# A two-layer encoder trunk: reads for a half's second part queued behind the weights, activations rounded behind their weight tile, one activation table loaded later

## The chip, the cores and the metric

One core of one Trainium2 chip. The metric is the device time of one execution in microseconds (us). The program is built by a tile framework whose scheduler decides, from a timeline of its own, in which order each engine's instructions stand; `issue_after(x)` in the source adds the condition that what follows stands behind `x` in time. What the scheduler made of the source is shown below where it matters.

## The reference

`x` is 512 tokens of 1024 floats. Layer 0 mixes by a convolution and a gated linear attention, layer 1 by softmax attention with forget gates; each layer ends with a PEER expert block, which is where most of the work is:

```python
def peer_ffn(h, wq, keys, u, v):              # h: 512 x 1024, u and v: 16384 x 1024
    q = h @ wq                                # 8 heads, two halves of 128
    s1, s2 = q[..., 0, :] @ keys[:, 0], q[..., 1, :] @ keys[:, 1]
    v1, i1 = top_k(s1, 16); v2, i2 = top_k(s2, 16)
    sc, j = top_k(v1[:, None] + v2[None, :], 16)          # 16 experts a head, 128 a token
    experts, gates = i1[j // 16] * 128 + i2[j % 16], softmax(sc)
    act = gelu(u[experts] . h)
    return sum(gates * act * v[experts])
```

`x = x + mix(rms_norm(x))` and `x = x + peer_ffn(rms_norm(x))` in each of the two layers.

## The kernel before, in words

The program runs `mix_even`, `peer(0)`, `mix_odd` and `peer(1)` one after the other. Each `peer` treats 128 tokens (block 0) by gathering the rows of `u` and `v` that its tokens chose, and the other 384 tokens densely: for all 16384 experts, in 128 tiles of 128.

The dense part has two halves. The **u half** (`u_step`, L842) loads a weight tile of 128x1024 floats, computes 24 matmuls into a PSUM bank `pu`, takes the gelu of it, and keeps the 128x384 activations: the last 24 tiles in SBUF (`act0` to `act23`), the first 104 in DRAM (`aside`). Beside it `gate4` builds the tokens' gates and writes them to DRAM as `G`. The **v half** (`prepare`, L962, and `v_sweep`, L1022) takes each tile's gates (`gc`, read from `G` for 8 tiles at once) and activations (kept, or `at`, read from `aside` for 2 tiles at once), multiplies them on VectorE (L971), and uses the product as the stationary operand of 18 matmuls with the weight tile of `v`.

Every operand in float32 is split into two float32r parts (`split`, L49): ScalarE rounds it (`whi` for a weight, `wh` for the gated activations, both L50), and VectorE (in places GpSimd) takes the rest (`wlo`, `wl`, both L51). Buffers: 4 `raw` weight tiles in flight, 3 each of `whi`, `wlo`, `wh`, `wl`, 2 of `gc`, 3 of `at`. All weight loads (L58), `gc` (L957) and `at` reads (L960) go through one queue, SP's, in one order.

The v half's order of experts is such that the 24 kept tiles come first. When the u half's last gates are done (about 12 tiles before its end), `upool` is closed, the pools of the v half are opened, and `fetch` (L950) is called for the first tiles: that asks for two `gc` and three `at` reads at once. Inside the loop it is called four tiles ahead.

Gathers go on in both halves on GpSimd's queue (L861 and L872); VectorE takes their dot products (L863) and later their weighted sum (L874). When the last dot product is there, `g_w` (L866) takes its gelu on ScalarE.

`mix_odd` begins with a request to load ScalarE's table set that holds both exp and ln (L545), placed behind `last_gelu`, which is `g_w`'s gelu. In the attention, `log_sigmoid` (L206 to L218) uses exp (L211) and ln (L215), `rsqrt` (L223, L224) ln and then exp, and the softmax exp (L645). `sums_in` (L588) transposes the result of `log_sigmoid`, `fz`, on TensorE (L590); `normalise` (L617) ends in `ka` or `qa` (L627), which the logits (L639) need.

Of the kernel before, what the change touches and what calls it, by code (L numbers as in the profile page):

```python
# [39 lines left out]
TAIL = 12  # L40
NEG = -3.0e38
# [3 lines left out]
class Trunk:  # L45
# [8 lines left out]
    def weight(self, src, shape=None, eng=None, after=None):  # L54

        nc = self.nc
        raw = self.ws.tile([P, D], F32, tag="raw", name="raw", bufs=4)
        nc.sync.dma_start(raw, src)  # L58
        hi = self.ws.tile([P, D], F32R, tag="whi", name="whi", bufs=3)
        lo = self.ws.tile([P, D], F32R, tag="wlo", name="wlo", bufs=3)  # L60
        if after:
            with self.tc.issue_after(after.ins):
                self.split(raw, hi, lo, eng)
        else:
            self.split(raw, hi, lo, eng)
        if shape:
            a, b = shape
            hi = hi.rearrange("p (a b) -> p a b", a=a)
            lo = lo.rearrange("p (a b) -> p a b", a=a)
        return hi, lo  # L70
# [471 lines left out]
    def mix_odd(self):  # L542
        nc, tc, A = self.nc, self.tc, self.A
        with tc.issue_after(self.last_gelu.ins):
            nc.scalar.preload_act_table_set("natural_log_exp_and_others")  # L545
        hT = self.new_hT()
        with tc.tile_pool(name="m1c", bufs=1) as sc:
            start, rest = self.nat_parts(A["w_v1"][0], self.rows(hT), 2, eng=nc.gpsimd)
            self.rms_h(2, hT, after=start)
            self.mix_odd_body(hT, sc, rest)  # L550
# [263 lines left out]
    def peer_body(self, L, hT, h0, sp, sb):  # L814
# [27 lines left out]
        def u_step(e, eng=None):  # L842
# [10 lines left out]
            self.last_gelu = nc.scalar.activation(a, p, AF.Gelu)  # L853
# [96 lines left out]
        def fetch(n):  # L950
# [3 lines left out]
            if m % EC == 0 and m < NE1:  # L954
                e = order[m]
                gcs[m] = vb.tile([P, NTG, EC * TG], F32, name="gc")
                nc.sync.dma_start(gcs[m], G[:, :, e * TG:(e + EC) * TG].rearrange("g p n -> p g n"))  # L957
            if 0 <= n < NE1 and (e := order[n]) < NE1 - KEEP and n % 2 == 0:
                ats[n] = vb.tile([P, 2, TD], F32, name="at", bufs=3)
                nc.sync.dma_start(ats[n], aside[e:e + 2].rearrange("e p t -> p e t"))  # L960

        def prepare(n):  # L962
# [5 lines left out]
            lo = self.last_lo  # L968
# [5 lines left out]
            self.split(w, *[t.rearrange("p (g t) -> p g t", t=TG) for t in (wh, wl)])  # L974
# [13 lines left out]
        while nu < NE1:  # L988
# [15 lines left out]
            if not (gates or products or vb):  # L1004
                upool.__exit__(None, None, None)
                vb = vpool.__enter__()
                for n in range(-AHEAD, AHEAD):
# [52 lines left out]
    def build(self, stop=4, first=0):  # L1060
        nc, tc, A = self.nc, self.tc, self.A
        with tc.tile_pool(name="const", bufs=1) as cp, tc.tile_pool(name="ws", bufs=1) as self.ws, \
# [13 lines left out]
            self.last_gelu = nc.vector.memset(sc[:, 0:1], -0.5)  # L1076
# [97 lines left out]
```

## Time and profile before

| | us |
|---|---|
| median of 3 runs | 3146.25 (3145.14 to 3149.17) |
| the profiled execution | 3148.14 |
| its span, from the first instruction to the last | 3146.3 |
| TensorE busy in the span | 3080.9 |
| VectorE, ScalarE, GpSimd busy | 2406.8, 1437.2, 1155.1 |
| moved by DMA | 787.16 MB, 250 GB/s on average |

All times in rows are from the start of the span. Layer 0's u half ends at about 1012 us, its v half at 1540, the attention at 1868; layer 1's u half ends at 2609, its v half at 3138. PE is TensorE, DVE VectorE, ACT ScalarE, POOL GpSimd, SPq the queue of DMA issues on SyncE. A row of idle time names what the engine's next instruction waited for last.

### The profile page before, as it was taken

What the parts mean: (1) busy time and instruction counts of PE and PEld (TensorE: products, weight loads), DVE (VectorE), ACT (ScalarE), POOL (GpSimd) and SP (SyncE); (2) the same over time, 40 slices, a digit from 0 to 9 for tenths busy, and PEclk for the clock granted to TensorE, in tenths of its full rate; (3) what the DMA queues carried; (4) which work ended last, traced back from release to release, by engine and by line L of the source; (5) the groups of instructions that cost most, each with busy time, mean ns of one, the idle gap of its engine ahead of it and who ended that gap; (6) DMA issues with size and microseconds to landing.
All of it is one profiled execution on the core that took longest, in us unless ns stands there. A gap on an engine that the chain in (4) does not pass through costs nothing.

```text
span 3146.3 us, 45733 instructions
## 1 busy us (share of the span) xinstructions
PE 3080.9 (98%) x15932; PEld 2696.8 (86%) x15932; DVE 2406.8 (76%) x4936; ACT 1437.2 (46%) x2258; POOL 1155.1 (37%) x800
## 2 busy tenths in 40 slices
PE   8999999999999999999999999999999999999999
PEld 6668999999999888877766679999999998888787
DVE  6765998888885888888535548998888867888786
ACT  4343334666664333333356633336666643333332
POOL 1220122996773332332100000227976752233330
PEclk9999999999999999999999999999999999999999
DMA  4113445999998999999421124448999997999996
GB/s 155 54 34 125 137 140 168 358 351 347 339 323 292 310 350 372 352 350 356 148 81 41 41 77 132 137 144 313 375 340 339 339 322 260 354 367 346 355 349 233
DMA packets 334202, 787.16 MB, mean 250 GB/s; under 512 B 26745, under 2 KB 181770, under 8 KB 327826
## 3 DMA queue, kind: packets, MB, share of 16 engines
q1 hardware_dynamic: 260242, 515.76, 47.0%
q0 software_dynamic: 73728, 268.47, 24.1%
q8 instruction: 125, 2.05, 0.3%
q14 instruction: 107, 0.88, 0.1%
HBM read 687.59 MB, written 96.47 MB: 249 GB/s over the span
## 4 chain that ended last, share of the span: by engine, by line
PE 90%; DVE 3%; DMA 2%; issue 1%; ACT 1%; SPq 1%; POOL 1%; DVEq 0%; ACTq 0%; POOLq 0%
PE acc L1027 33%; PE pu L79 10%; PE pu L78 10%; PE pu L77 10%; PE bank L77 5%; PE bank L79 5%; PE bank L78 5%; PE bank L911 5%; PE po L671 1%; PE pc L284 1%; PE bank L639 1%; PE bank L935 1%; DVE wlo L51 1%; SPq L960 1%; POOL gr L861 1%
## 5 line engine op out<-in xcount | busy, mean ns | idle before, releaser
L50 ACT ACTIVATE whi<-raw 128x1024 fp32r<-128x1024 f32 x604 | 636.9, 1057 | 829.5 <-PE pu L78 471.6
L51 DVE TENSOR_TENSOR wlo<-raw,whi 128x1024 fp32r<-128x1024 f32 x565 | 692.1, 1226 | 183.1 <-ACT whi L50 156.3
L77 PE MATMUL pu<-hhi,whi 128*128 128x384 f32 x2048 | 702.0, 343 | 9.6 <-ACT whi L50 8.7
L79 PE MATMUL pu<-hhi,wlo 128*128 128x384 f32 x2048 | 691.0, 338 | 2.2 <-DVE wlo L51 2.2
L78 PE MATMUL pu<-hlo,whi 128*128 128x384 f32 x2048 | 689.2, 337 | 0.0
L872 POOL DMA_INDIRECT gr<-in_vF_dram,ids x256 | 317.7, 1241 | 717.7 <-DVE x L874 658.7
L1027 PE MATMUL acc<-wlo,wh 128*128 128x512 f32 x1536 | 472.7, 389 | 0.0
L1027 PE MATMUL acc<-whi,wl 128*128 128x512 f32 x1536 | 472.5, 389 | 0.0
L1027 PE MATMUL acc<-whi,wh 128*128 128x512 f32 x1536 | 436.5, 390 | 9.3 <-ACT whi L50 9.3
L861 POOL DMA_INDIRECT gr<-in_uN_dram,ids x256 | 352.5, 1377 | 237.6 <-DVE dots L863 140.7
L50 ACT ACTIVATE wh<-gc 128x384 fp32r<-128x384 f32 x256 | 134.4, 525 | 645.7 <-PE acc L1027 638.0
L77 PEld LDWEIGHTS pu<-hhi,whi 128*128 128x128 f32 x2048 | 388.3, 190 | 12.1 <-ACT whi L50 9.3
L79 PEld LDWEIGHTS pu<-hhi,wlo 128*128 128x128 f32 x2048 | 387.3, 189 | 4.0 <-DVE wlo L51 3.9
L78 PEld LDWEIGHTS pu<-hlo,whi 128*128 128x128 f32 x2048 | 388.1, 190 | 1.9 <-DVE hlo L117 0.6
L1027 PEld LDWEIGHTS acc<-whi,wh 128*128 128x128 f32 x1536 | 287.6, 188 | 72.1 <-ACT whi L50 12.6
L1027 PEld LDWEIGHTS acc<-wlo,wh 128*128 128x128 f32 x1536 | 288.3, 188 | 60.0
L1027 PEld LDWEIGHTS acc<-whi,wl 128*128 128x128 f32 x1536 | 288.3, 188 | 59.8
L901 POOL TENSOR_SCALAR a<-cst,sT 128x128 f32<-128x128 f32 x192 | 330.6, 1722 | 13.2 <-PE bank L911 4.9
L874 DVE SCALAR_TENSOR_TENSOR x<-gr,dots,x 128x1024 f32<-128x1024 f32 x256 | 327.4, 1279 | 0.3
L863 DVE CUSTOM_DVE_ANT_0 gr<-gr,h 128x1024 f32<-128x1024 f32 x256 | 307.9, 1221 | 23.8 <-DMA gr<-in_uN_dram,ids 23.7
L51 DVE TENSOR_TENSOR wl<-gc,wh 128x384 fp32r<-128x384 f32 x256 | 142.7, 558 | 179.4 <-ACT wh L50 170.0
L51 POOL TENSOR_TENSOR wlo<-raw,whi 128x1024 fp32r<-128x1024 f32 x39 | 99.0, 2540 | 398.5 <-ACT whi L50 390.5
(248 smaller groups left out, 4242.3 us busy)
## 6 DMA issues: line engine op xcount, KB each, us to landing
raw<-in_uT_dram SPq DMA_DIRECT2D x256, 512.0 KB
raw<-in_vF_dram SPq DMA_DIRECT2D x256, 512.0 KB
G<-big SPq DMA_DIRECT2D x48, 1024.0 KB
gc<-G SPq DMA_DIRECT2D x32, 1536.0 KB
aside<-xact SPq DMA_DIRECT2D x208, 192.0 KB
at<-aside SPq DMA_DIRECT2D x104, 384.0 KB
raw<-in_w_in_dram SPq DMA_DIRECT2D x32, 512.0 KB
raw<-in_wq_dram SPq DMA_DIRECT2D x32, 512.0 KB
```

The source lines that it names most:

```text
L50: first = self.nc.scalar.activation(hi, raw, AF.Copy)
L51: self.last_lo = (eng or self.nc.vector).tensor_tensor(lo, raw, hi.bitcast(F32), op=ALU.subtract)
L77: mm(out, lh, rh, start=first, stop=False)
L78: mm(out, lh, rl, start=False, stop=False)
L79: return mm(out, ll, rh, start=False, stop=last)
L861: nc.gpsimd.indirect_dma_start(out=r, out_offset=None, in_=uN, in_offset=bass.IndirectOffsetOnAxis(ap=ids[:, s:s + 1], axis=0))
L863: return lambda: nc.vector.tensor_tensor_reduce(r, r, h0, 1.0, 0.0, ALU.mult, ALU.add, accum_out=dots[:, s:s + 1])
L872: nc.gpsimd.indirect_dma_start(out=r, out_offset=None, in_=vF, in_offset=bass.IndirectOffsetOnAxis(ap=ids[:, s:s + 1], axis=0))
L874: return lambda: nc.vector.scalar_tensor_tensor(self.x0, r, dots[:, s:s + 1], self.x0, op0=ALU.mult, op1=ALU.add)
L901: (nc.vector if t else nc.gpsimd).tensor_scalar(a1[:, t], self.iota, e1[:, t:t + 1], gate[:, t:t + 1], op0=ALU.is_equal, op1=ALU.mult)
L911: nc.tensor.matmul(p[:, t], a2[:, t], a1[:, t], start=True, stop=True)
L1027: nc.tensor.matmul(acc[b][c], wt[:, s], vt[:, c], start=(n == 0 and wt is wh and vt is vh), stop=(n == NE1 - 1 and wt is wl))
```

## The change

Three things are done. `fetch` is called seven tiles later than the pools are opened (`SETTLE`), and each `gc` and `at` read is asked to stand behind the last weight load issued by then. The split of the gated activations (`wh`, `wl`) is asked to stand behind the rounding of its own tile's weights. The table set of the attention is asked to be loaded behind the u half's last gelu (`last_act`) as well as behind `g_w`'s.

```diff
+SETTLE = 7
...
         raw = self.ws.tile([P, D], F32, tag="raw", name="raw", bufs=4)
-        nc.sync.dma_start(raw, src)
+        self.last_raw = nc.sync.dma_start(raw, src)
...
         if after:
             with self.tc.issue_after(after.ins):
-                self.split(raw, hi, lo, eng)
+                self.last_hi = self.split(raw, hi, lo, eng)
         else:
-            self.split(raw, hi, lo, eng)
+            self.last_hi = self.split(raw, hi, lo, eng)
...
-        with tc.issue_after(self.last_gelu.ins):
+        with tc.issue_after(self.last_gelu.ins), tc.issue_after(self.last_act.ins):
             nc.scalar.preload_act_table_set("natural_log_exp_and_others")
...
-            self.last_gelu = nc.scalar.activation(a, p, AF.Gelu)
+            self.last_act = nc.scalar.activation(a, p, AF.Gelu)
...
                 gcs[m] = vb.tile([P, NTG, EC * TG], F32, name="gc")
-                nc.sync.dma_start(gcs[m], G[:, :, e * TG:(e + EC) * TG].rearrange("g p n -> p g n"))
+                with tc.issue_after(self.last_raw.ins):
+                    nc.sync.dma_start(gcs[m], G[:, :, e * TG:(e + EC) * TG].rearrange("g p n -> p g n"))
...
                 ats[n] = vb.tile([P, 2, TD], F32, name="at", bufs=3)
-                nc.sync.dma_start(ats[n], aside[e:e + 2].rearrange("e p t -> p e t"))
+                with tc.issue_after(self.last_raw.ins):
+                    nc.sync.dma_start(ats[n], aside[e:e + 2].rearrange("e p t -> p e t"))
...
-            lo = self.last_lo
+            lo, hi = self.last_lo, self.last_hi
...
-            self.split(w, *[t.rearrange("p (g t) -> p g t", t=TG) for t in (wh, wl)])
+            with tc.issue_after(hi.ins):
+                self.split(w, *[t.rearrange("p (g t) -> p g t", t=TG) for t in (wh, wl)])
...
                 vb = vpool.__enter__()
+                opened = nu
+            if vb and nu == opened + SETTLE:
                 for n in range(-AHEAD, AHEAD):
                     fetch(n)
...
-            self.last_gelu = nc.vector.memset(sc[:, 0:1], -0.5)
+            self.last_gelu = self.last_act = nc.vector.memset(sc[:, 0:1], -0.5)
```

SP's queue at the end of layer 1's u half, from the last write of `G` on (`raw<-in_uT` is a weight tile of the u half, `raw<-in_vF` one of the v half), before:

```order
L914 DMA G<-big 128x2048
L58 DMA raw<-in_uT_dram 128x1024 x2
L957 DMA gc<-G 128x24x128 x2
L960 DMA at<-aside 128x2x384 x3
L58 DMA raw<-in_uT_dram 128x1024 x2
L58 DMA raw<-in_vF_dram 128x1024
L58 DMA raw<-in_uT_dram 128x1024
L58 DMA raw<-in_vF_dram 128x1024 x10
L957 DMA gc<-G 128x24x128
L58 DMA raw<-in_vF_dram 128x1024 x8
```

and in the changed kernel:

```order
L915 DMA G<-big 128x2048
L59 DMA raw<-in_uT_dram 128x1024 x2
L959 DMA gc<-G 128x24x128
L59 DMA raw<-in_uT_dram 128x1024 x2
L59 DMA raw<-in_vF_dram 128x1024
L59 DMA raw<-in_uT_dram 128x1024
L59 DMA raw<-in_vF_dram 128x1024
L959 DMA gc<-G 128x24x128
L59 DMA raw<-in_vF_dram 128x1024 x10
L959 DMA gc<-G 128x24x128
L59 DMA raw<-in_vF_dram 128x1024 x8
L963 DMA at<-aside 128x2x384
```

One `gc` read instead of two, and no `at` read, now stands between the last two weight loads that follow `G` and the u half's last three. The second `gc` has moved behind the v half's second weight tile, the three `at` reads behind its 20th, 22nd and 24th. Layer 0 differs only by four small loads of the attention in between. Later in the half each `at` and `gc` stands one weight load further back than before.

ScalarE in the middle of layer 0's v half (numbers tell the buffers apart: `whi_12385`, `_12417`, `_12451`, `_12485` are the rounded weights of tiles 80 to 83, `wh_12390`, `_12422`, `_12456`, `_12490`, `_12524` the rounded gated activations of tiles 80 to 84), before:

```order
L50 ACTIVATE wh_12422<-gc_12112 128x384
L50 ACTIVATE whi_12385<-raw_12383 128x1024
L50 ACTIVATE wh_12456<-gc_12112 128x384
L50 ACTIVATE whi_12417<-raw_12415 128x1024
L50 ACTIVATE wh_12490<-gc_12112 128x384
L50 ACTIVATE wh_12524<-gc_12112 128x384
L50 ACTIVATE whi_12451<-raw_12449 128x1024
L50 ACTIVATE whi_12485<-raw_12483 128x1024
```

and in the changed kernel:

```order
L51 ACTIVATE whi_12385<-raw_12383 128x1024
L51 ACTIVATE wh_12390<-gc_12112 128x384
L51 ACTIVATE whi_12417<-raw_12415 128x1024
L51 ACTIVATE wh_12422<-gc_12112 128x384
L51 ACTIVATE whi_12451<-raw_12449 128x1024
L51 ACTIVATE wh_12456<-gc_12112 128x384
L51 ACTIVATE whi_12485<-raw_12483 128x1024
L51 ACTIVATE wh_12490<-gc_12112 128x384
```

Before, `wh` had run one tile ahead of `whi`, and here two tiles: the activations of tiles 83 and 84 stand ahead of the weights of tile 82. The place with two `wh` and then two `whi` occurs four times in each layer's v half; in the changed kernel each `wh` stands right behind its own tile's `whi`.

ScalarE where the attention takes the log of its forget gates (`ls_e`, `ls_u` and `ls_l` are the steps of `log_sigmoid`, `sq` the squares of a projection), before:

```order
L210 ACTIVATE ls_e<-fz 16x512
L211 ACT_TABLE_LOAD
L211 ACTIVATE ls_e<-ls_e 16x512
L215 ACT_TABLE_LOAD
L215 ACTIVATE ls_l<-ls_u 16x512
L50 ACTIVATE whi<-raw 128x1024
L614 ACTIVATE sq<-bank 128x512
```

and in the changed kernel:

```order
L211 ACTIVATE ls_e<-fz 16x512
L212 ACTIVATE ls_e<-ls_e 16x512
L216 ACTIVATE ls_l<-ls_u 16x512
L51 ACTIVATE whi<-raw 128x1024
L615 ACTIVATE sq<-bank 128x512
```

Before, the requested load stood ahead of the u half's last gelus, so the gelu's set was loaded again and the attention began with it; from there each ln and each exp of `rsqrt` loaded another set. In the changed kernel the one requested load stands behind the last gelu, and no other load follows until layer 1's first gelu. Of the program's 47 table loads 13 are left.

## Rows read from the trace of the kernel before

**Rows 1.** The page: busy us, share of the span and instructions of each engine.

```profile
PE 3080.9 (98%) x15932; PEld 2696.8 (86%) x15932; DVE 2406.8 (76%) x4936; ACT 1437.2 (46%) x2258; POOL 1155.1 (37%) x800
```

**Rows 2.** Who TensorE waited for over the whole span: us in total, times, longest.

```profile
PE acc L1027 <- ACT whi L50: 9.3, 8, 1.2
PE pu L77 <- ACT whi L50: 8.7, 2, 4.4
PE bank L639 <- issue: 3.6, 1, 3.6
...
PE bank L590 <- ACT sq L614: 2.1, 1, 2.1
```

**Rows 3.** The timeline of SP's queue at the end of layer 1's u half: start, length of the issue (of all that the row counts together), what is issued.

```profile
2566.90 8.57 SPq L957 DMA_DIRECT2D gc<-G  x2
2586.67 1.71 SPq L58 DMA_DIRECT2D raw<-in_uT_dram  x2
```

**Rows 4.** The chain of work that ended last: start, length, what. First the issues at the end of layer 0's u half (the second `gc`, the first `at`), then the load at the end of layer 1's, from issue to landing.

```profile
971.22 5.61 SPq L957
976.88 12.74 SPq L960
...
2586.67 9.55 DMA raw<-in_uT_dram
```

**Rows 5.** The timeline there, of ScalarE, VectorE and GpSimd: two gelus of finished u tiles (L853), the rounding that waited for the load, the gelu of the dot products (L867), the last two dot products but one, and the last gather of u's rows.

```profile
2584.68 0.49 ACT L853 ACTIVATE act<-pu 128x384 f32<-128x384 f32 x1 [2.90 <-PE pu L79]
2588.84 0.49 ACT L853 ACTIVATE act<-pu 128x384 f32<-128x384 f32 x1 [3.67 <-PE pu L79]
2596.30 1.06 ACT L50 ACTIVATE whi<-raw 128x1024 fp32r<-128x1024 f32 x1 [6.97 <-DMA raw<-in_uT_dram]
...
2583.73 1.22 DVE L863 CUSTOM_DVE_ANT_0 gr<-gr,h 128x1024 f32<-128x1024 f32 x1
...
2571.60 0.95 POOL L861 DMA_INDIRECT gr<-in_uN_dram,ids  x1 [0.60 <-DVE dots L863]
```

**Rows 6.** TensorE's timeline where it resumed, in layer 0 and in layer 1.

```profile
1001.45 0.69 PE L77 MATMUL pu<-hhi,whi 128*128 128x384 f32 x1 [4.22 <-ACT whi L50]
...
2597.41 0.69 PE L77 MATMUL pu<-hhi,whi 128*128 128x384 f32 x1 [4.45 <-ACT whi L50]
```

**Rows 7.** Stretches behind TensorE's idle times of 4.22, 4.45, 2.12 and 3.62 us: the stretch and its us, busy us (instructions) of PE, PEld, DVE, ACT and POOL, TensorE's granted clock as a share of full, the DMA engines' busy share, GB/s.

```profile
1001.45:1006.30 4.85, 4.60 (x14) 4.09 (x14) 4.38 (x7) 3.58 (x6) 1.95 (x1) 0.51 0.53 168
...
2597.41:2603.60 6.19, 5.94 (x17) 5.43 (x18) 5.37 (x8) 3.22 (x5) 1.69 (x1) 0.50 0.63 216
...
1589.99:1596.70 6.71, 6.71 (x19) 5.32 (x20) 1.45 (x2) 0.00 (x0) 0.00 (x0) 0.50 0.25 82
...
1801.65:1812.90 11.25, 11.24 (x35) 6.53 (x35) 5.54 (x16) 2.96 (x9) 0.00 (x0) 0.55 0.01 1
```

**Rows 8.** The timeline of ScalarE and then TensorE at one of the eight short waits of the v halves, the roundings of the order shown above; under them the stretch behind it, with the columns of rows 7.

```profile
1346.96 0.52 ACT L50 ACTIVATE wh<-gc 128x384 fp32r<-128x384 f32 x1 [2.60 <-PE acc L1027]
1351.04 0.52 ACT L50 ACTIVATE wh<-gc 128x384 fp32r<-128x384 f32 x1 [3.56 <-PE acc L1027]
1351.47 1.99 ACT L50 ACTIVATE whi<-raw 128x1024 fp32r<-128x1024 f32 x2
...
1352.56 0.50 PE L1027 MATMUL acc<-whi,wh 128*128 128x512 f32 x1 [1.16 <-ACT whi L50]
...
1353.00:1360.00 7.00, 7.00 (x33) 5.73 (x32) 7.00 (x8) 1.94 (x3) 2.99 (x2) 1.00 0.79 248
```

**Rows 9.** ScalarE's table loads by line: count, busy us, mean ns, idle time before.

```profile
L224 ACT ACT_TABLE_LOAD x16 | 20.5, 1283 | 0.3
L223 ACT ACT_TABLE_LOAD x15 | 19.2, 1283 | 0.3
```

**Rows 10.** The timeline of ScalarE, VectorE and TensorE at `log_sigmoid`.

```profile
1585.82 1.28 ACT L215 ACT_TABLE_LOAD   x1
1585.84 0.41 DVE L212 TENSOR_SCALAR ls_u<-ls_e 16x512 f32<-16x512 f32 x1 [1.18 <-ACT ls_e L211]
1587.12 0.63 ACT L215 ACTIVATE ls_l<-ls_u 16x512 f32<-16x512 f32 x1
1589.21 0.68 DVE L218 TENSOR_TENSOR fz<-fz,ls_u 16x512 f32<-16x512 f32 x1
1589.99 0.57 PE L590 MATMUL bank<-cst,fz 16*128 16x16 f32 x4 [2.12 <-ACT sq L614]
```

**Rows 11.** The same three engines at the last `normalise`, and TensorE at a short wait early in the attention with the stretch behind it.

```profile
1796.86 1.28 ACT L223 ACT_TABLE_LOAD   x1
1801.65 0.76 PE L639 MATMUL bank<-ka,qa 66*128 66x128 f32 x2 [3.62 <-issue]
...
1634.80 0.48 PE L658 MATMUL bank<-cst,pr 128*128 128x128 f32 x1 [1.43 <-DVE pr L647]
...
1635.00:1640.00 5.00, 5.00 (x17) 3.41 (x17) 1.57 (x7) 4.25 (x6) 0.00 (x0) 0.74 0.22 81
```

**Rows 12.** Who waited for DMA in layer 0's v half: ScalarE's roundings in all, and the longest; then the whole v half as a stretch, with the columns of rows 7.

```profile
ACT whi L50 <- DMA raw<-in_vF_dram: 4.6, 5, 1.4
...
1189.77 1.06 ACT L50 ACTIVATE whi<-raw 128x1024 fp32r<-128x1024 f32 x1 [1.41 <-DMA raw<-in_vF_dram]
...
1012.00:1540.00 528.00, 523.37 (x2311) 432.66 (x2310) 430.89 (x513) 193.31 (x259) 151.52 (x124) 1.00 0.95 331
```

## The prediction

> **What bounds the kernel now.** I read the page first: TensorE is busy 3080.9 of 3146.3 us, the next engine 76% [rows 1]. So the time is TensorE's work plus what it idles, 65 us, plus what it loses at half clock after idling. The list of its waits comes next [rows 2]: 9.3 us in eight equal waits of the v halves for `whi`, 8.7 us in two long waits of the u halves for `whi`, and in the attention one of 3.6 and one of 2.1 us. These are the four places that the change touches. Then each place in the timeline, to see what came last, and the stretch behind it, for the granted clock. The sum is made against the profiled execution, 3148.1 us, which is 1.9 us above the median of 3146.25.
>
> **Part 1, reads at the u half's end.** In layer 1 the two `gc` issues take SP's queue 8.57 us from 2566.90 on [rows 3]. It is the DMA behind a `gc` that is held: in layer 0 the second `gc` 5.61 us, the `at` behind that 12.74 [rows 4]. So one `gc` costs its successor 6 to 13 us, with nothing but weight loads ahead of it 6 to 8. Only then, at 2586.67, goes the load of u tile 125, which lands 9.55 us later [rows 4]; ScalarE rounds it at 2596.30, having sat idle for it [rows 5], and TensorE resumes at 2597.41 after 4.45 us (layer 0: 1001.45, 4.22 us) [rows 6]. It resumes at half clock: granted 0.51 for 4.85 us in layer 0 and 0.50 for 6.19 us in layer 1 [rows 7]. Half of the busy time there, 2.30 and 2.97 us, and the 0.25 us of idling in each (the stretch less the busy time) are lost too. That makes 4.22+2.55=6.8 and 4.45+3.22=7.7, together 14.4 us.
>
> After the change one `gc` stands ahead of this load. It goes out at about 2566.90, when `G` has landed as before, and holds the load until about 2575.5; with the old 9.55 us the tile lands at 2585. A u step takes 4.16 us (two gelus of finished tiles are that far apart, 2584.68 and 2588.84 [rows 5]); tile 124 ends at 2592.96, so tile 125 is wanted, with 1.06 us for its rounding, by 2591.9. It is some 7 us early; in layer 0, let through at 976.8 as the second `gc` was and landed by 986.4 against 996.2, some 10. The bound from the other side: if nothing were gained, 0 of the 14.4. I take all of it, since the landing time is that of a load with two `gc` and three `at` ahead of it, and now less is ahead. What is late next: the second `gc`, now behind v tile 1, holds v tile 2 for 8 us, from some 2587 to 2596, landing by 2606. That tile is wanted at 2592.96 plus three u steps and two v steps of 4.08 (two `wh` of rows 8 are that far apart), 2613.6. The other `gc` reads have kept their place within one tile. The `at` reads come four tiles ahead of use, 16 us, against the same 9.55. `g_w`'s gelu also moves, ahead of two u roundings: ScalarE then waits for the last dot product. The last gather of u rows is issued at 2571.60 and the dot product before it runs at 2583.73 [rows 5], so the gelu can go by about 2586, and u tile 126's rounding behind it is not wanted before 2596.
>
> **Part 2, roundings in the v halves.** At 1351.04 `wh` runs after 3.56 us of waiting for TensorE, and the two `whi` behind it start only then; TensorE wants the first one and idles 1.16 us [rows 8]. The order of the instructions says why: `wh` two tiles ahead stands in front, and its buffer comes free only when the tile before the wanted one is done. Right behind its own `whi`, `wh` waits for nothing later than `whi` itself does. A pair takes 1.06+0.52 us [rows 5, 8] at the start of the three tiles' time (12 us) that the buffers give, so nothing new is late. All eight go: 9.3 us [rows 2]; the clock was 1.00 behind them [rows 8], so there is no more to get. Bounds: 0 and 9.3.
>
> **Part 3, the table.** The attention's 31 loads of `rsqrt` [rows 9] and two of `log_sigmoid` [rows 10], 1.28 us each, go from ScalarE: 42 us of its time, nearly all beside TensorE's work. On the path they stand twice.
>
> At `log_sigmoid`, exp is 1.28 us earlier, and ln follows VectorE's `ls_u` (0.41 us from 1585.84 [rows 10]) instead of the second load: 1585.84-1.28+0.41, with 0.05 for the hand-over 1585.02, instead of 1587.12, 2.1 us earlier. The rest of the chain is fixed, so `fz` is done at 1587.8 instead of 1589.9, and TensorE, free at 1589.99-2.12=1587.87, does not wait. Its clock was 0.50 for the 6.71 us that followed [rows 7]: another 3.36. Together 5.5 us.
>
> At the last `normalise`, two loads of 1.28 us lie in the 3.62 us that TensorE waits [rows 11]: 2.6 us go, 1.05 stay. Behind it the granted clock was 0.55 for 11.25 us [rows 7]. If the clock holds and only TensorE limits, up to 0.45 x 11.24 = 5.1 us more; if it falls all the same, 0. The nearest rows disagree: after 1.16 us in the v half it held at 1.00 [rows 8], after 1.43 us in this attention it fell to 0.74 over the next 5 us [rows 11]. I take the middle, 2.5, also because the softmax's own chain through VectorE fills part of that stretch.
>
> The one load that stays, behind the u half's last gelu, fits into ScalarE's 3.56 us of idling a tile [rows 8].
>
> The Trainium skill, ScalarE: Activation LUTs, section Rules for kernel authors, has one budget about 2.7 us for each switch of the set. By that the wait of 3.62 us would go altogether and the sum would be 1.05 us larger. The rows have 1.283 us for every load [rows 9], and the sum goes by them.
>
> **Sum.** 14.4 + 9.3 + 5.5 + 2.6 + 2.5 = 34.3 us. 3148.1 - 34.3 = 3113.8 against the profiled execution; 1.9 less against the median: **3112 us**, 1.1% faster. About 0.2%, 6 us, is what a measurement of this kernel can tell from no change.
>
> **Rivals.**
>
> A. The front wait shrinks but stays. For: one `gc` is still ahead of the load, and DMA is as full as before. Against: 7 to 10 us of room. Price: half of the 14.4 us stays, so 3119.
>
> B. The v halves keep short waits, because ScalarE, its rounding of weights first, now meets another wait in front, such as a late load. For: the roundings already wait for DMA, 4.6 us in layer 0, up to 1.41 at a time [rows 12]. Against: none of these reached TensorE, and weight loads now go ahead of each `at`. Price: 9.3 us kept, 3121.
>
> C. The reads come late and the kernel is slower. Each `gc` and `at` is asked for later; in the v half the DMA engines are busy 0.95 of the time [rows 12]. VectorE multiplies by `gc` and `at` ahead of the next `wlo`, so one late read holds the weights too. If each of the 30 later `gc` reads (15 a layer after its first) ended in a wait of TensorE of 1.41 us [rows 12], 42.3 us would be lost against 34.3 gained: 3112+42.3=3154, slower than before. It decides from 1.15 us a read on (34.3/30). Against: there are 8 us of room at the second `gc` and 16 us of lead at each `at`.
> The Trainium skill, DMA: Bandwidth & Descriptors, section Rules for kernel authors, has one issue a DMA early and wait late; by that rule the change goes the wrong way, and this rival is what it would do here. The waits of rows 2 speak against it as far as they go: in them it is the early reads that stand in front of what TensorE needs.
>
> D. The change doesn't do what it says in the attention: `fz`'s chain is held by something else and the clock falls as before. For: part 3's two places hang on short chains through three engines. Price: 5.5+2.6+2.5=10.6 us kept, 3123.
>
> **How the numbers follow.** Forecast 0.70: its terms are read off rows, and only the clock term (0 to 5.1) is open, so 3109 to 3115, and some 3 us more to either side for the profile's roundings. A 0.12, B 0.09, D 0.05, C 0.04. The range reaches from the forecast's fast end past A, B and D: 3106 to 3124, and leaves out C and joint cases of A, B and D. Faster by over 0.2%: 0.94 (forecast, A, B and D, less 0.02 for A, B and D coming together). Within 0.2%: 0.03 (these 0.02, and 0.01 of C in a milder form). Slower: 0.03, C.
>
> **What would show it.** In the profile after: no wait of `pu` for `whi` at the two u halves' ends, and granted clock 1.00 there; SP's load of u tile 125 issued within 9 us of the first `gc`; no wait of `acc` for `whi`; no table load between `mix_odd`'s one and layer 1's first gelu; no wait at L590's line; at the last `normalise` a wait near 1 us. Wrong if `acc` waits for `wh` or VectorE for `at` or `gc` (C), or if a wait for a load stays at the front (A).

## The result, and the profile after

The changed kernel's first executions took 3103.41 (profiled), 3106.19 and 3108.55 us against a median of 3145.69 us before: a ratio of 0.9873, 95% interval 0.9853 to 0.9892, faster by 1.27%. One more execution, of 4920.68 us at a mean granted clock of 0.623, is left out. 0.9873 x 3145.69 is 3105.7 us: the direction and the mechanism are the prediction's, the gain is 40 us instead of 34.3, and the time lies 6.3 us below the forecast, 0.3 us outside the range. Half a microsecond of that comes from the lower median before (3145.69 now, 3146.25 in the prediction); the 5.7 us in the gain do not.

The page after, busy us of the engines, answers to [rows 1]: TensorE has 22.2 us less of busy time for the same matmuls, as less of them runs at half clock, and idles 42.9 us where it had idled 65.4.

```profile
span 3101.6 us, 45719 instructions
...
PE 3058.7 (99%) x15932; PEld 2684.7 (87%) x15932; DVE 2401.2 (77%) x4936; ACT 1384.7 (45%) x2224; POOL 1096.6 (35%) x800
```

Who TensorE waited for, over the whole span, answers to [rows 2]. The waits of `acc` and of `pu` for `whi` and the one for `sq` are gone; the wait at the last `normalise` is 0.4 us, not the 1.05 predicted. What leads the list lies at the two layers' fronts, which the change was not about.

```profile
PE bank L115 <- DVE xs L108: 12.8, 3, 10.4
PE bank L115 <- DVE ss L106: 4.5, 2, 2.8
...
PE bank L640 <- issue: 0.4, 1, 0.4
```

The timeline of the changed kernel at four places. At the end of layer 1's u half, SP issues one `gc`, then the loads of tiles 125 and 126, and both are through 8.4 us behind it ([rows 3] had 19.8 us between the first `gc` and the start of that load). At `mix_odd`'s front VectorE takes an `hlo` and then an `xs` of 3.40 us, beside a `wlo` on GpSimd. At `log_sigmoid` ln follows `ls_u` without a load and the first `fz` matmul without a wait ([rows 10]). At the last `normalise` ln and exp stand back to back ([rows 11]).

```profile
2536.34 0.38 SPq L959 DMA_DIRECT2D gc<-G  x1
2539.34 5.41 SPq L59 DMA_DIRECT2D raw<-in_uT_dram  x2
...
1532.51 1.29 DVE L118 TENSOR_TENSOR hlo<-bank,hhi 128x512 fp32r<-128x512 f32 x2 [0.99 <-ACT hhi L117]
...
1535.38 3.40 DVE L108 SCALAR_TENSOR_TENSOR xs<-x,rs,grow 128x1024 f32<-128x1024 f32 x1 [1.20 <-POOL rs L107]
1535.31 2.39 POOL L52 TENSOR_TENSOR wlo<-raw,whi 128x1024 fp32r<-128x1024 f32 x1
...
1567.08 0.41 DVE L213 TENSOR_SCALAR ls_u<-ls_e 16x512 f32<-16x512 f32 x1
1567.52 0.63 ACT L216 ACTIVATE ls_l<-ls_u 16x512 f32<-16x512 f32 x1 [0.51 <-DVE ls_u L213]
...
1570.39 0.39 PE L591 MATMUL bank<-cst,fz 16*128 16x16 f32 x4
...
1772.09 0.68 ACT L224 ACTIVATE rs<-bank,sc 128x512 f32<-128x512 f32 x1
1772.80 0.63 ACT L225 ACTIVATE rs<-rs 128x512 f32<-128x512 f32 x1
1773.46 1.53 DVE L628 SCALAR_TENSOR_TENSOR ka<-bank,qkg,rs 64x512 f32<-64x512 f32 x2 [0.55 <-ACT rs L225]
1774.31 0.46 PE L640 MATMUL bank<-ka,qa 66*128 66x128 f32 x2 [0.41 <-issue]
```

Stretches of the changed kernel, with the columns of [rows 7]: the two u halves' ends, the middle of layer 0's v half, and the stretches behind the first `fz` matmul and behind the last `normalise`. The clock is 1.00 in all of them ([rows 7] had 0.51, 0.50, 0.50 and 0.55).

```profile
980.00:1012.00 32.00, 32.00 (x180) 31.22 (x179) 16.48 (x25) 12.47 (x20) 5.78 (x4) 1.00 0.85 294
2545.00:2580.00 35.00, 35.00 (x196) 33.99 (x195) 18.11 (x24) 14.00 (x21) 7.45 (x6) 1.00 0.85 292
1100.00:1500.00 400.00, 400.00 (x1766) 331.35 (x1765) 336.09 (x400) 145.00 (x197) 107.31 (x101) 1.00 1.01 359
...
1570.39:1577.10 6.71, 6.71 (x30) 4.93 (x31) 1.45 (x2) 2.12 (x3) 0.00 (x0) 1.00 0.26 81
...
1774.30:1785.60 11.30, 10.67 (x54) 6.26 (x55) 8.87 (x29) 5.71 (x18) 0.00 (x0) 1.00 0.01 1
```

**Four stretches to compare by.** Each runs from one instruction to another that all the kernels have, so its length counts standing still and half clock alike. *Tail and v half*: from ScalarE's gelu of u tile 120 to the end of the last `acc` matmul. *Front*: from there to the first `fz` matmul. *Middle*: from the first softmax transpose (`bank<-cst,pr`) to the last `ka,qa` matmul after a wait. *Behind*: from there to layer 1's first `bank<-cst,xs`. In us:

| kernel (profile) | tail and v half, layer 0, 1 | front | middle | behind |
|---|---|---|---|---|
| before | 563.65, 564.46 | 44.92 | 166.85 | 68.91 |
| before, second profile | 565.14, 564.47 | 43.36 | 165.50 | 69.00 |
| part 1 alone | 556.51, 556.51 | 43.38 | 165.62 | 69.05 |
| part 2 alone | 557.59, 557.25 | 42.34 | 165.60 | 69.04 |
| part 3 alone | 563.88, 563.82 | 42.87 | 162.28 | 64.07 |
| the change | 550.62, 550.62 | 40.25 | 162.40 | 64.08 |
| the change, second profile | 550.62, 550.62 | 40.24 | 164.03 | 64.08 |

How such a length is read, in rows: gelu of tile 120 and last `acc` matmul in layer 0, of the kernel before (1544.44+0.62-981.42 = 563.64)

```profile
981.42 0.47 ACT L853 ACTIVATE act<-pu 128x384 f32<-128x384 f32 x1
...
1544.44 0.62 PE L1027 MATMUL acc<-whi,wl 128*128 128x512 f32 x2
```

and of part 1 alone (1535.09+0.62-979.19 = 556.52).

```profile
979.19 0.47 ACT L854 ACTIVATE act<-pu 128x384 f32<-128x384 f32 x1
...
1535.09 0.62 PE L1032 MATMUL acc<-whi,wl 128*128 128x512 f32 x2
```

### The profile page after: what moved, and what is told of

It reads as the page before. It is cut to its first block, busy times and chain, and to the rows that moved or that the text cites. A ratio compares the mean times of both kernels' runs of the same rounds, so it can differ in the third digit from the quotient of the medians.

```text
span 3101.6 us, 45719 instructions
## 1 busy us (share of the span) xinstructions
PE 3058.7 (99%) x15932; PEld 2684.7 (87%) x15932; DVE 2401.2 (77%) x4936; ACT 1384.7 (45%) x2224; POOL 1096.6 (35%) x800
## 4 chain that ended last, share of the span: by engine, by line
PE 92%; DVE 3%; issue 2%; DMA 1%; POOL 1%; ACT 1%; DVEq 0%; POOLq 0%; ACTq 0%
PE acc L1033 32%; PE pu L79 11%; PE pu L80 11%; PE pu L78 11%; PE bank L78 6%; PE bank L80 5%; PE bank L79 5%; PE bank L912 5%; PE pc L285 1%; PE po L672 1%; PE bank L640 1%; PE bank L936 1%; DMA gr<-in_uN_dram,ids 1%; DVE wlo L52 1%; PE bank L659 1%
## 5 line engine op out<-in xcount | busy, mean ns | idle before, releaser
L873 POOL DMA_INDIRECT gr<-in_vF_dram,ids x256 | 277.0, 1082 | 720.8 <-DVE x L875 696.2
L1033 PE MATMUL acc<-wlo,wh 128*128 128x512 f32 x1536 | 439.2, 389 | 0.0
L1033 PE MATMUL acc<-whi,wl 128*128 128x512 f32 x1536 | 436.8, 389 | 0.0
L902 POOL TENSOR_SCALAR a<-cst,sT 128x128 f32<-128x128 f32 x192 | 316.3, 1648 | 15.2 <-PE bank L912 5.6
L899 DVE TENSOR_TENSOR a<-cst,sT 128x512 f32<-128x512 f32 x192 | 133.4, 695 | 126.2 <-PE bank L912 114.8
L78 PE MATMUL bank<-hhi,whi 128*128 128x512 f32 x512 | 211.5, 414 | 3.5 <-DVE hlo L118 2.7
```

The lines of the kernel that those rows point to most:

```text
L78: mm(out, lh, rh, start=first, stop=False)
L873: nc.gpsimd.indirect_dma_start(out=r, out_offset=None, in_=vF, in_offset=bass.IndirectOffsetOnAxis(ap=ids[:, s:s + 1], axis=0))
L902: (nc.vector if t else nc.gpsimd).tensor_scalar(a1[:, t], self.iota, e1[:, t:t + 1], gate[:, t:t + 1], op0=ALU.is_equal, op1=ALU.mult)
L1033: nc.tensor.matmul(acc[b][c], wt[:, s], vt[:, c], start=(n == 0 and wt is wh and vt is vh), stop=(n == NE1 - 1 and wt is wl))
```

## The experiments

Theory 1 was that each part is worth more than the prediction made it; theory 2, that its sizes hold and the rest of the 44.7 us between the two profiled executions is chance. Ratios below are to the runs of the kernel before on the same chip.

**The three parts, each alone, and the whole again.** Part 1 alone keeps these edits of the change

```diff
+SETTLE = 7
+                with tc.issue_after(self.last_raw.ins):
                     nc.sync.dma_start(gcs[m], ...
+                with tc.issue_after(self.last_raw.ins):
                     nc.sync.dma_start(ats[n], ...
+                opened = nu
+            if vb and nu == opened + SETTLE:
```

> Only part 1: the reads for the v half are asked for seven tiles later and behind a weight load; the order of the roundings and the table's place are those of the kernel before. By the prediction's sizes 14.4 us go (3131.3 against 3145.7). By the difference of the two traces, counted from the start of one matmul to the start of the next, 16.8 us go: at each u half's end some 5.0 us of standing still and 3.4 us at half clock. So theory 1 (the waits were read too small, because idle time is counted from the modelled end of a matmul) expects 3129 and theory 2 (the prediction's sizes hold, and what is over is chance of the profiled execution) 3131. Both expect no pu wait for whi at the ends of the u halves, the eight short waits of acc for whi still there, the waits at log_sigmoid and at the last normalise as before, and clock 0.5 behind these.

Measured: 3129.95 us, 0.9955 (0.9941 to 0.9968), 14 us, which can't tell the two theories apart. The u halves' waits are gone, the eight short ones are there. In its stretches, the middle of the v half has 25 matmuls fewer than the changed kernel has in the same 400 us; behind the first `fz` matmul, which waited 2.12 us as before, the clock is 1.00 this time; behind the last `normalise` it is 0.55 again.

```profile
1100.00:1500.00 400.00, 395.37 (x1741) 326.01 (x1740) 332.75 (x393) 144.46 (x194) 123.47 (x100) 1.00 1.00 353
...
1579.10:1585.80 6.70, 6.70 (x30) 4.91 (x31) 1.36 (x2) 0.83 (x1) 0.00 (x0) 1.00 0.25 81
1786.50:1797.80 11.30, 11.29 (x35) 6.28 (x35) 5.45 (x16) 2.96 (x9) 0.00 (x0) 0.55 0.01 1
```

By the table part 1 is worth (563.65-556.51)+(564.46-556.51) = 15.1 us, against 14.4 predicted and 16.8 by theory 1. Against the second profile of the kernel before it is 16.6, and between part 2 alone and the whole change 13.6: the two waits are not equally long in every execution (3.7 to 5.0 us).

Part 2 alone keeps

```diff
-            self.split(w, ...
+            with tc.issue_after(hi.ins):
+                self.split(w, ...
```

> Only part 2: the gated activations are rounded behind their own tile's weights. By the prediction 9.3 us go (3136.4). By the traces the eight waits cost 1.32 us each, not 1.16, counted from start to start: 10.6 us. And the order of this kernel shows something the prediction did not look at: at the front of mix_odd VectorE now has the first hlo ahead of the second xs, as in the changed kernel; there the wait of 2.92 us and 3.41 us at half clock were gone, worth 2.6 us. Theory 1 expects 13 us (3132.5) and no half clock at mix_odd's front, theory 2 9.3 us (3136.4) with the half clock there as before.

Measured: 3129.66 us, 0.9958 (0.9944 to 0.9971), 13 us. The order at `mix_odd`'s front is the new one: an `hlo` stands ahead of the second `xs`. In the kernel before it stood behind, and TensorE waited for it (first row, of the kernel before).

```profile
1551.76 0.50 PE L79 MATMUL bank<-whi,hlo 128*128 128x512 f32 x1 [2.92 <-DVE hlo L117]
...
1537.64 1.29 DVE L118 TENSOR_TENSOR hlo<-bank,hhi 128x512 fp32r<-128x512 f32 x2 [1.00 <-ACT hhi L117]
...
1540.51 3.40 DVE L108 SCALAR_TENSOR_TENSOR xs<-x,rs,grow 128x1024 f32<-128x1024 f32 x1 [1.19 <-POOL rs L107]
```

Its stretches: the v half's full count of matmuls, the clock at `mix_odd`'s front 1.00, and behind the 2.12 us at `log_sigmoid` 0.75 (before 0.50, in part 1 alone 1.00).

```profile
1100.00:1500.00 400.00, 400.00 (x1767) 331.31 (x1766) 338.92 (x403) 145.28 (x198) 110.15 (x101) 1.00 1.00 358
1535.30:1545.00 9.70, 6.37 (x40) 5.15 (x39) 7.28 (x10) 5.08 (x9) 9.01 (x5) 1.00 0.46 146
1577.60:1584.30 6.70, 6.69 (x25) 5.36 (x26) 1.36 (x2) 0.00 (x0) 0.00 (x0) 0.75 0.23 81
```

The v halves' gain is cleanest between part 1 alone and the whole change: 2 x (556.51-550.62) = 11.8 us. The front is 43.38-42.34 = 1.0 us shorter than in part 1 alone, neither with any half clock.

Part 3 alone keeps

```diff
-        with tc.issue_after(self.last_gelu.ins):
+        with tc.issue_after(self.last_gelu.ins), tc.issue_after(self.last_act.ins):
...
-            self.last_gelu = nc.scalar.activation(a, p, AF.Gelu)
+            self.last_act = nc.scalar.activation(a, p, AF.Gelu)
```

> Only part 3: the table set is loaded behind the u half's last gelu. By the prediction 10.6 us go (3135.1): 5.5 at log_sigmoid, 2.6 at the last normalise and 2.5 of the 5.1 us that the half clock behind it costs. By the traces 5.8 at log_sigmoid and 8.6 at the last normalise, where the wait fell from 3.62 to 0.41 us and the clock held: 14.4 us (3131.3). Theory 1: the wait at the last normalise is 0.4 us and the clock behind it 1.00. Theory 2: about 1 us stays, or the clock falls behind it again. The half clock at mix_odd's front should stay under both, since VectorE's order there is that of the kernel before.

Measured: 3135.02 us, 0.9968 (0.9956 to 0.998), 10 us. The wait at the last `normalise` is 0.40 us and the clock behind it 1.00, as theory 1 had it. That the time is the prediction's 3135.1 is luck: the last `normalise` gives 8.0 us instead of 5.1 and `log_sigmoid` 2.1 instead of 5.5 (the table of the next section). At `mix_odd`'s front, where the old order and its wait of 2.9 us stand, the clock is 0.79.

```profile
1550.00:1558.00 8.00, 5.81 (x23) 4.67 (x24) 5.27 (x7) 0.59 (x2) 4.29 (x3) 0.79 0.56 193
...
1792.10:1803.40 11.30, 10.67 (x54) 6.26 (x55) 8.87 (x29) 5.72 (x18) 0.00 (x0) 1.00 0.01 1
```

> The whole change once more, for its size and for a second profile. Theory 1 (the three parts are worth 16.8, 13 and 14.4 us) expects the sum, 44 us less what half clock shows up elsewhere, 3102 to 3106. Theory 2 (part of the 44.7 us was chance of the profiled execution) expects 3108 to 3112, with half clock in some of the places where the first profile had none: at 574 us, at mix_odd's front, behind the wait of 1.4 us early in the attention.

Measured: 3104.24 us, 0.9873 (0.9858 to 0.9888), 35 to 45 us, in theory 1's range. Half clock showed up at one of the places named, behind the wait of 1.42 us early in the attention (clock 0.66):

```profile
1611.60:1616.60 5.00, 5.00 (x16) 3.38 (x17) 3.05 (x9) 1.81 (x4) 0.00 (x0) 0.66 0.23 90
```

The parts' ratios add up to 37.5 us (14.2+13.2+10.1), the whole is 40.0; with intervals of 4 us to either side they agree.

**The clock behind the last `normalise`.** The prediction had put it between 0 and 5.1 us and taken 2.5. Two kernels bring a wait back there and leave everything else as in the changed kernel. The first restores both loads:

```diff
                     normalise(hp, w)
+                    if (hp, w) == (7, 0):
+                        with tc.issue_after(self.last_exp.ins):
+                            nc.scalar.preload_act_table_set("exp_and_others")
```

> The whole change, but exp's own table set is asked for once behind the exp of the last normalise but one, so that the last one switches the set for ln and again for exp, as before the change: two loads of 1.28 us on its chain, everything else as in the changed kernel. Theory 1 (the last normalise was worth 3.2 us of wait and all of the half clock behind it, 8.6 us in all): the wait grows from 0.41 to 2.97 us, TensorE stands at half clock for 10.24 us behind it as in the three profiles that had 3.62 us, and the kernel takes 2.6+5.1=7.7 us longer than the whole change, 3112. Theory 2 (the prediction's middle: the clock is worth half of its 5.1 us, since VectorE fills the stretch): 2.6 to 5 us longer, 3107 to 3109.

Measured: 3113.03 us, 0.9892 (0.9876 to 0.9909). By the ratios that is 6 us over the whole change, by the medians, from two chips, 8.8. The row is TensorE's where it resumes,

```profile
1777.47 0.46 PE L640 MATMUL bank<-ka,qa 66*128 66x128 f32 x2 [3.10 <-issue]
```

and this the stretch behind it, with the clock as low as in [rows 7]:

```profile
1777.50:1788.70 11.20, 11.20 (x34) 6.09 (x35) 5.41 (x16) 2.96 (x9) 0.00 (x0) 0.54 0.01 1
```

"Middle" is 165.09 us instead of 162.40 and "behind" 69.03 instead of 64.08, together 7.6 us where theory 1 had 7.7. So behind this wait all of the half clock counts, 4.95 us, and VectorE's chain hid next to none of it. Theory 1 holds here. The second kernel has one load:

```diff
+        ln = nc.scalar.activation(dst, src, AF.Ln, bias=self.epsc)
+        if load:
+            with self.tc.issue_after(ln.ins):
+                table = nc.scalar.preload_act_table_set("exp_and_others")
+            with self.tc.issue_after(table.ins):
+                self.last_exp = nc.scalar.activation(dst, dst, AF.Exp, scale=-0.5)
...
+                self.rsqrt(rs, pn, (hp, w) == (7, 1))
```

> The whole change, but with one table load between ln and exp of the last normalise. Both theories: the wait is 0.41+1.28=1.69 us. Theory 1 (a wait of 3 us or more is followed by half clock every time, one of 1.4 to 2.1 us only in some executions: 1 of 6 behind the 1.42 us early in the attention, 2 of 3 behind the 2.12 us at log_sigmoid) leaves open whether the clock falls here: 3106 without it, 3108 to 3111 with it. Theory 2 (any wait over 1 us lets it fall in this stretch, where TensorE's matmuls are few): half clock for 3.4 us or more behind it.

Measured: 3108.81 us, 0.9881 (0.9864 to 0.9897). TensorE waits 1.68 us,

```profile
1775.86 0.46 PE L646 MATMUL bank<-ka,qa 66*128 66x128 f32 x2 [1.68 <-issue]
```

and the clock stays at 1.00, with 54 matmuls where two loads left 34:

```profile
1775.90:1787.10 11.20, 10.57 (x54) 6.21 (x55) 8.77 (x28) 5.66 (x18) 0.00 (x0) 1.00 0.01 1
```

Theory 2 falls for this execution; one profile can't say that it falls for every one. The load itself costs 1.3 us ("middle" 163.69 instead of 162.40). The profiled execution took 3108.04 us where theory 1 had 3106 without half clock; it is longer than the change's first profile mostly in layer 1's u half ahead of the tail (711.0 against 707.9 us), which the edit does not touch.

**Which reads held tile 125.** Each kernel is the changed one without one of the two ties to a weight load.

```diff
-                with tc.issue_after(self.last_raw.ins):
-                    nc.sync.dma_start(gcs[m], ...
+                nc.sync.dma_start(gcs[m], ...
```

> The whole change, but the gc reads are not tied to a weight load: two of them stand again ahead of the load of u tile 125, with no at read. Theory 1 (it is the DMA behind a gc that is held, 5.6 us behind the first and 12.7 behind the second, and the three at reads only add their 0.4 us each): the load goes out some 1.2 us earlier than in the kernel before, TensorE waits 3.0 to 3.5 us at both u halves' ends with half clock behind it, and the kernel takes 2 x (3.3+3.4)=13 us longer than the whole change, 3117. Theory 2 (the at reads were as much to blame): no wait over 1 us there, 3104.

Measured: 3112.4 us, 0.9895 (0.9878 to 0.9911), but 3103.45 in the profiled execution, which has no wait there. Its three other executions, 3111.6 to 3114.5 us, have no profile, and where they lost their time is not known. The working behind theory 1's number was wrong: the load of tile 125 behind the two `gc` is let through 16.4 us after that of tile 124 (20.8 in the kernel before, 8.8 in the changed one, all at layer 1's end), so the three `at` reads had held it for another 4 us here, not for 0.4 each. ScalarE rounds the tile at 2559.39, having waited for it, and TensorE does not notice.

```profile
2559.39 1.06 ACT L51 ACTIVATE whi<-raw 128x1024 fp32r<-128x1024 f32 x1 [5.05 <-DMA raw<-in_uT_dram]
```

> The kernel with two gc reads in front once more: its profiled execution of 3103.45 us had no wait at the u halves' ends, with tile 125 rounded less than 2 us ahead of its need, while its three other executions took 3111.6 to 3114.5 us. Theory 1 (it is at the edge: in most executions tile 125 lands too late, a wait of 1 to 3 us and half clock of 3.4 us each follow): a profile of an execution over 3110 us shows these waits. Theory 2 (the longer executions lost their time elsewhere): no wait there in a profile of over 3110 us.

Measured: 3109.32 us, 0.9881 (0.9864 to 0.9897); the profiled execution took 3110.49. It has two waits at layer 1's end, far less than theory 1's,

```profile
2567.98 0.45 PE L78 MATMUL pu<-hhi,whi 128*128 128x384 f32 x1 [0.54 <-ACT whi L51]
...
2569.24 0.45 PE L80 MATMUL pu<-hhi,wlo 128*128 128x384 f32 x1 [0.64 <-DVE wlo L52]
```

and "tail and v half" at 550.84 and 552.35. So it sits at the edge and loses up to 1.7 us there. The rest of this execution's 7.1 us over the change's first profile lies elsewhere (theory 2), in places that the edit does not touch: 1.6 us in the attention and 4.0 in layer 1's u half ahead of its tail. The load of tile 125 is let through 19.2 and 18.7 us after that of tile 124 here, so the share of the `at` reads differs from execution to execution: over both layers' ends it is 17.6 us on average with two `gc` alone (4 cases) and 20.5 with the `at` reads as well (8 cases), some 3 us more. The other tie:

```diff
-                with tc.issue_after(self.last_raw.ins):
-                    nc.sync.dma_start(ats[n], ...
+                nc.sync.dma_start(ats[n], ...
```

> The whole change, but the at reads are not tied to a weight load: one gc and three at stand ahead of the load of u tile 125. Theory 1 (one gc holds the queue 6 to 8 us, the at reads cost 0.4 us each of the queue and 1.2 MB of transfer ahead of the tile, some 3.6 us at the 330 GB/s of the v half): the tile lands 2 us or more ahead of its need, no wait at the u halves' ends, 3104. Theory 2 (the at reads were as much to blame): a wait of 1 to 4 us at both ends and half clock behind it, 3110 to 3118.

Measured: 3107.24 us, 0.9878 (0.9862 to 0.9895); no wait, "tail and v half" 550.87 and 550.62, as theory 1 had it. So the tie of the `gc` reads is enough to keep the tile in time. The tie of the `at` reads alone takes nearly all of the wait away but leaves the tile at the edge; both together give the room. `SETTLE` does nothing: with 0 in its place the order of every engine is the same, row for row, as the tie alone already holds the reads back.

**Late reads, the rival on the other side.**

```diff
-AHEAD = 4
+AHEAD = 2
```

> The whole change, but gc and at reads are asked for two tiles ahead of their place instead of four. This is the rival of late reads with its condition made harder. By the prediction's working: an at read then has 8.2 us of lead against a landing of 9.55 us, so it comes 1.4 us late or more, and the product ahead of the next wlo waits for it; half of the 52 at reads of a layer late by 1.4 us, if each reached TensorE, would be 2 x 26 x 1.4 = 73 us, 3180. If the three buffers of whi and wlo cover a late product (they hold two tiles, 8 us), VectorE waits but TensorE does not: 3104 to 3108. Which of the two decides how far the whole change is from the rival's side.

Measured: 3107.4 us, 0.9879 (0.9863 to 0.9896). With half the lead VectorE waits in layer 1's v half for nothing that is read (the first row is its ordinary wait for ScalarE), and TensorE has no wait at all in either v half. The rival was far from its point.

```profile
DVE wlo L52 <- ACT whi L51: 88.5, 110, 3.6
DVE x L1062 <- PE acc L1033: 6.7, 2, 4.9
DVE wl L52 <- ACT wh L51: 0.7, 1, 0.7
```

**A better version?**

```diff
-            start, rest = self.nat_parts(A["w_v1"][0], self.rows(hT), 2, eng=nc.gpsimd)
+            start, rest = self.nat_parts(A["w_v1"][0], self.rows(hT), 2)
```

> A candidate for a better version: the whole change, and the rests of mix_odd's first weights are taken by VectorE (1.22 us each) instead of GpSimd (2.4 to 2.85 us each). At mix_odd's front an xs on VectorE took 3.40 us beside GpSimd's work and 1.28 us without it, and TensorE waited 1.83 us for it. If that neighbour is the cause, xs takes 1.28 us and the wait of 1.83 us goes or shrinks, at the price of three times 1.22 us on VectorE ahead of it: between 1.8 us faster and 2 us slower than the whole change, from the end of the v half to the first fz matmul 38.5 to 42.3 us instead of 40.25.

Measured: 3108.08 us, 0.9884 (0.9868 to 0.9901), no better. The neighbour is the cause: without GpSimd's work the second `xs` takes 1.28 us.

```profile
1536.18 1.28 DVE L108 SCALAR_TENSOR_TENSOR xs<-x,rs,grow 128x1024 f32<-128x1024 f32 x1
```

But three `wlo` now stand on VectorE, and "front" is 39.95 us instead of 40.25. None of these kernels is better than the changed one; differences of a few us between them lie inside the intervals.

**The kernel before, a second profile.**

> The kernel before once more, for a second profile of it. Theory 1 (half clock follows a wait of 3 us or more every time, and one of 1 to 3 us by chance): half clock for 6.8 us behind both waits of 4.2 to 4.5 us at the u halves' ends and for 10.2 us behind the 3.62 us at the last normalise, as in the first profile; at 574 us, at mix_odd's front (2.92 us), at log_sigmoid (2.12 us) and behind the 1.43 us early in the attention not all of the four again. Theory 2 (each of these seven places has its half clock every time, and the whole gain of 44.7 us between the first two profiles belongs to the change): all seven again, with the same lengths.

Measured: 3144.73 us. The stretches behind the wait of 1.24 us at 572 us in layer 0's u half, of 5.00 us at that half's end, of 2.93 at `mix_odd`'s front, of 2.12 at `log_sigmoid`, of 1.42 early in the attention, of 3.62 at the last `normalise` and of 4.72 at layer 1's u half's end:

```profile
572.30:576.30 4.00, 4.00 (x23) 4.00 (x24) 4.00 (x8) 0.29 (x2) 3.84 (x3) 1.00 0.81 280
999.30:1004.20 4.90, 4.65 (x13) 4.14 (x14) 4.43 (x8) 3.68 (x6) 1.95 (x1) 0.50 0.45 145
1550.30:1556.00 5.70, 5.70 (x29) 4.79 (x30) 4.35 (x7) 1.09 (x2) 2.09 (x2) 1.00 0.59 208
1586.95:1593.65 6.70, 6.70 (x30) 4.92 (x31) 1.45 (x2) 0.83 (x1) 0.00 (x0) 1.00 0.23 82
1628.70:1633.70 5.00, 4.97 (x23) 3.83 (x24) 1.91 (x7) 4.48 (x6) 0.00 (x0) 1.00 0.25 88
1794.20:1805.50 11.30, 11.27 (x35) 6.55 (x35) 5.56 (x16) 2.96 (x9) 0.00 (x0) 0.55 0.01 1
2594.30:2600.50 6.20, 5.95 (x19) 5.44 (x20) 5.37 (x8) 3.22 (x5) 1.69 (x1) 0.56 0.59 206
```

The three long waits have their half clock again; behind the four shorter ones it did not fall. Theory 1.

## Why the prediction was right in kind and short in size

The three mechanisms are the ones that the prediction named, and of its waits only 0.4 us at the last `normalise` is left. What failed is the size of terms of its sum: the price of the eight short waits (9.3 predicted, 11.8 found) and the half clock behind the last `normalise` (2.5 and 4.9) above all, and the reordering at `mix_odd`'s front (at least 1.0), which it put at nothing without looking.

| step | predicted | found | from |
|---|---|---|---|
| part 1, u halves' ends | 14.4 | 15.1 | before against part 1 alone |
| part 2, v halves | 9.3 | 11.8 | part 1 alone against the change |
| part 2, `mix_odd`'s front | none | 1.0, and 0 to 1.7 of clock | part 1 alone against part 2 alone |
| part 3, `log_sigmoid` | 5.5 | 2.1, and 0 to 3.4 of clock | part 2 alone against the change |
| part 3, wait at the last `normalise` | 2.6 | 3.1 | "middle", 165.5 against 162.4 |
| part 3, clock behind it | 2.5 | 4.9 | "behind" |
| sum | 34.3 | 38.0, and 0 to 5.1 | measured 40.0 (34.0 to 46.2) |

**Part 1 was right**, in place and size (13.6 to 16.6 us, by the profiles compared). Tile 125's load goes out in time and nothing else became late: the second `gc`, the later ones and the `at` reads never reached TensorE, even with half the lead. The prediction reckoned only with what a `gc` holds up; the `at` reads behind it add some 3 us, as the kernels with one tie show.

**Part 2 failed in the price of a wait.** The eight waits were all found and all went, but 1.16 us was taken from the idle column. That column counts from the modelled end of the last matmul, 0.39 us after its start, while the next would have started 0.23 us after it. From start to start the wait took 1.54 us instead of 0.23 (the matmul ahead of it starts at 1351.02, it at 1352.56 [rows 8]), and the matmuls behind it need another 0.15 us until they are back in step (the first follows after 0.34 us, the next after some 0.235): 11.8/8 = 1.47 us each. Counted in matmuls it is nearly the same: 400 us of the v half hold 1741 with the four waits and 1766 without, 25 x 0.2267 = 5.7 us for four, 1.4 each. The Trainium skill, Perfetto Trace Analysis, section Tensor Engine Instruction (MATMUL, LD_WEIGHTS), says that the end of a TensorE instruction is a model and not a measurement; the trace agrees, since 0.39 us for every matmul that follows 0.23 us behind another can't all be its own time.

```profile
1351.02 0.39 PE L1027 MATMUL acc<-whi,wl 128*128 128x512 f32 x1
```

**The order of the front was not looked at.** Part 2 also moved VectorE's work at `mix_odd`'s front. The prediction followed the order of instructions at the places of its terms only; the new order there is worth 1.0 us, and the 2.92 us wait that it removed was followed by half clock in two of four profiles that had it.

**At the last `normalise` the middle was the wrong choice.** Of 0 to 5.1 us it took 2.5; 4.9 went. Of the two rows that disagreed neither was a neighbour: their waits were 1.16 and 1.43 us, the one here 3.62. In all five profiles with a wait of 3.1 to 3.6 us at this place the stretch behind it has the low clock, and in none of the nine with 0.4 or 1.7 us. The wait left is 0.41 us and not 1.05, since TensorE's own work ahead of it (the `sq` and `po` matmuls) now runs some 0.5 us later against ScalarE's softmax.

**At `log_sigmoid` the clock was taken as certain.** The wait of 2.12 us was worth 2.1 us. The 3.36 us of half clock behind it came from one execution; of four profiles with the same wait the first has 0.50, one 0.75 and two 1.00. On average that is 1.3 us, not 3.4.

The errors are of both signs: too little by 0.7, 2.5, 1.0, 0.5 and 2.4, too much by some 2 at `log_sigmoid`. The range held 3 us to the fast side for the profile's roundings, which is less than these. The 44.7 us between the two profiled executions are 26.9 in the tails and v halves, 17.2 in the attention and 0.6 elsewhere; some 6 of the attention's (325.5 against 319.6 us from the last `acc` matmul to layer 1's first `bank<-cst,xs` in the two profiles of the kernel before) are half clock that the second profile does not have. By that the first profile of the kernel before was an unlucky one, and the term of 3.4 us at `log_sigmoid` was read from it.

## What to carry to other kernels

Price a TensorE wait from start to start, or by the matmuls missing from a fixed stretch, not by the idle column. Count half clock in full at a place where every profile shows it, and as a chance behind a wait of 1 to 3 us that a single profile shows; the length of the wait alone does not tell the two apart. Compare the order of all instructions, not only where the change is meant to act: a reordering at a place that no edit names was worth 1 to 2.7 us here.

## What the runs showed of the hardware

Half clock behind short waits differs from execution to execution of the same program. The wait of 1.42 us early in the attention was the same in all 14 profiles of these kernels; behind it the clock fell in six and held in eight. Behind the 2.12 us at `log_sigmoid` and the 2.9 us at `mix_odd`'s front it fell in four of eight cases; behind 3.7 to 5.0 us at the u halves' ends in eight of eight. Length alone does not decide: at layer 1's front a wait of 2.8 us, shorter than the one at `mix_odd`'s front, has half clock at it in all 14 profiles, also in the changed kernel, where it is left (why this place differs is not shown).

```profile
1838.39 0.89 PE L115 MATMUL bank<-cst,xs 128*128 128x128 f32 x3 [2.79 <-DVE ss L106]
...
1838.39:1843.39 5.00, 4.65 (x25) 4.01 (x25) 4.35 (x7) 4.75 (x9) 2.66 (x3) 0.66 0.00 0
```

VectorE's `xs` over 128x1024 elements takes 1.28 us alone and 3.40 us when a `wlo` of the same size on GpSimd has started just ahead of it (1535.31 against 1535.38 in the changed kernel). Where `xs` started first, by 0.17 us, it took 1.28 us and the `wlo` 3.35 instead of 2.39, as in the kernel before (`xs` at 1543.67):

```profile
1543.84 3.35 POOL L51 TENSOR_TENSOR wlo<-raw,whi 128x1024 fp32r<-128x1024 f32 x1 [0.20 <-ACT whi L50]
```

Removing the neighbour gave VectorE the 2.1 us back, but not the kernel.
